# Opening of a two-layer decoder trunk: sums of squares with tokens on partitions, and the first weights split in two pieces

## Chip, cores, metric

The kernel runs on one core of one Trainium2 chip, in one launch. The metric is device time in microseconds (us). The engines are named as in the profile: PE (TensorE, matmuls; PEld are its weight loads), DVE (VectorE), ACT (ScalarE), POOL (GpSimd), SP (SyncE, which issues most transfers). "SPq" is SP's DMA queue.

## What is computed

A trunk of two layers on 512 tokens with 1024 features. Each layer normalizes its input, scales and shifts it by vectors computed from a conditioning vector c, projects it, mixes it three ways, and ends in a gated feed-forward part. The change concerns only the first normalization and the start of the first projection:

```python
c_act = silu(c)
mod = (c_act @ w_ada + b_ada)                   # six vectors of 1024: sh1, sc1, g1, sh2, sc2, g2
h = rmsnorm(x, norm1_w) * (1 + sc1) + sh1       # x * rsqrt(mean(x*x) + EPS) * norm1_w ...
u = h @ w_in                                    # the input projection
q = u[..., 1024:1536]                           # one of its parts; pool and conv inputs are others
```

## The kernel before

*Layout.* Features lie on partitions and tokens along the free axis: `x[k]` is slice k of the features (128 of 1024, k = 0 to 7) by 512 tokens. Weights arrive in blocks of 128x128 in the order in which they are used.

*Precision.* Every product is made of three matmuls in a reduced float format (`F32R`): an operand is split into a high half (rounded) and a low half (the rest), and `mm3` adds high x high, high x low and low x high. For weights `split_w` makes the halves: `whi` on ACT (line 402), then `wlo` on DVE (line 405). For the activations of the first normalization `first_scaled` (line 638, DVE) multiplies x by the column `am` and the row `rstd`, `first_hi` (line 642, ACT) adds the shift and rounds, `first_lo` (line 645, DVE) makes the low half.

*The opening.* While x arrives, `c` is turned into a column of silu values and spread to a row on all partitions (`csil`) by eight transposes (line 163 is the helper). PE runs idle matmuls (`WARM`, `WARM2`, on `ones`) between. Then, slice by slice, squares are made on DVE and ACT, pairs are added on DVE (line 881), and a matmul with a 128x128 matrix of ones sums over the partitions, so that the sum of squares of every token stands on all partitions. ACT takes the reciprocal root y of the 128x512 sums (line 888) and a scaled square of it (line 889); DVE makes the Newton step from them in two instructions (lines 893, 894), which leaves `rstd` (with a negative sign; `minus` and `abias` carry the sign to the other side).

*Modulation.* For each slice j, `ada_first` makes two dots of 1024 elements with `csil` on DVE (line 482, each followed by the read of its accumulator), for the scale (SC1) and the shift (SH1), and finishes them on ACT: `am` (line 506) and `mod` (line 509). The rows of the matrix for it come by `ada_first_load`, two transfers of 512 KB for each slice; six tiles hold them.

*Weights of the first loop.* For each slice k the loop over k reads one chunk of 7 blocks (448 KB): four blocks for q and three for other inputs. In the loop a step has 21 matmuls: four token tiles of q with three each, then three feature tiles with three each. Three `raw` tiles hold chunks on arrival.

*Order.* Each engine runs its queue in order. The order is that of the compiler's plan: an instruction wrapped in `pin` stays behind everything that was written before it for its engine; the others (the `whi` splits, `am` and `mod` of slices from 1 on, `first_hi`, the transfers) are placed where the plan takes their operands to be ready. `tc.issue_after(ins)` puts an instruction behind `ins` in the queue of the same engine; it is no wait. `split_after` and `fetch_after` hold such marks: the split of a slice's weights stands behind the previous slice's `first_hi` on ACT; the fetches, which SP issues, are marked behind DVE instructions (`step`).

Of the kernel before, what the change touches and what calls it, by code (L numbers as in the profile page):

```python
# [12 lines left out]
F32 = mybir.dt.float32  # L13
F32R = mybir.dt.float32r
BF16 = mybir.dt.bfloat16
I32 = mybir.dt.int32
AF = mybir.ActivationFunctionType
ALU = mybir.AluOpType
# [3 lines left out]
P = 128  # L22
D = 1024
S = 512
L = 2
KT = D // P
# [3 lines left out]
TT = S // P  # L30
# [5 lines left out]
BLOCK = 256  # L36
DFF = 2816
NF = DFF // P
EPS = 1e-6
NEG = -1e30  # L40
SCALE = 1.0 / math.sqrt(HD)
C_BLOCKS = 8
# [13 lines left out]
C_N1, C_N2, C_ADA, C_PS, C_CW = 0, 8, 16, 64, 66  # L56
# [9 lines left out]
SH1, SC1, G1, SH2, SC2, G2 = range(6)  # L66
# [9 lines left out]

WARM = 9

WARM2 = 19

GATE2 = ([("gate", j) for j in range(6)] + [("attn", 0), ("attn", 1), ("gate", 6), ("gate", 7)]
         + [("attn", j) for j in range(2, 8)])
# [3 lines left out]
def hybrid_trunk(ctx, tc, xT, ws, ada, cols, pool_w, qk_w, crow, pos, con, out):  # L86
    nc = tc.nc
    V, A, T = nc.vector, nc.scalar, nc.tensor

    const = ctx.enter_context(tc.tile_pool(name="const", bufs=1))  # L90
    big = ctx.enter_context(tc.tile_pool(name="big", bufs=BIG))
    wp = ctx.enter_context(tc.tile_pool(name="wp", bufs=4))
# [6 lines left out]
    def nm(s):  # L99
        uid[0] += 1  # L100
        return f"{s}{uid[0]}"

    def bigt(dt=F32R):
        return big.tile([P, S], dt, tag="big", name=nm("big"))
# [13 lines left out]
    def sm(shape, dt=F32, tag="sm", bufs=8):  # L118
        return small.tile(shape, dt, tag=tag, name=nm(tag), bufs=bufs)

    f32 = lambda ap: ap.bitcast(F32)
# [34 lines left out]
    def matmul(*a, **k):  # L156
        tc.keep_in_program_order(T.matmul(*a, **k))  # L157

    def pin(ins):
        return tc.keep_in_program_order(ins)  # L160

    def transpose(*a):
        tc.keep_in_program_order(T.transpose(*a))  # L163
# [11 lines left out]
    def cut(pair, *ix):  # L175
        return pair[0][ix], pair[1][ix]

    def table(func, after):

        A.activation(sm([P, 1], tag="tab", bufs=1), after, func)  # L180
# [6 lines left out]
    x = [const.tile([P, S], F32, name=f"x{k}") for k in range(KT)]  # L187
    colt = const.tile([P, L, NCOL], F32, name="colt")
# [15 lines left out]
    ident = const.tile([P, P], F32, name="ident")  # L204
# [3 lines left out]
    ones = f32(ones_r)  # L208
# [4 lines left out]
                            base=0, pattern=[[-1, P]], channel_multiplier=1)  # L213
    epst = const.tile([P, 1], F32, name="epst")
    nc.gpsimd.memset(epst, EPS)

# [20 lines left out]
    def fetch(tile, l, blocks):  # L239
        for i, n, src in runs(l, blocks):  # L240
            nc.sync.dma_start(tile[:, i:i + n].rearrange("p b n -> p (b n)"), src)
# [134 lines left out]
    items = []  # L376
    for l in range(L):
# [8 lines left out]
        for blocks in first_part + list(feed_forward()):  # L386
            if not isinstance(blocks, list):
                if isinstance(blocks, int):
                    blocks = GateUp(l, blocks)
# [3 lines left out]
    at = [0, 0]  # L393
    loaded = deque()
    hold, dots_after, last_split, scaled = [None], [None], [None], [None]

    def rawt():
        return wp.tile([P, C_BLOCKS, P], F32, tag="raw", name=nm("raw"), bufs=RAW)
# [33 lines left out]
    split_after, last_hi = [None], [None]  # L432

    fetch_after = [None]

    def load_w():
        while at[1] < min(at[0] + 1 + SUMS_AHEAD, len(items)):
            sums, sub = items[at[1]]
            if sums is not None and sub == 0:
                sums.begin()  # L440
            at[1] += 1
        sums, what = items[at[0]]
        at[0] += 1
        if sums is not None:
            return sums.load(what)
        l, blocks = what
        raw = rawt()
        with tc.issue_after(fetch_after[0].ins) if fetch_after[0] is not None else nullcontext():
            fetch(raw, l, blocks)
        if by_transfer(l, blocks):  # L450
            return split_by_transfer(raw, l, blocks)
        with tc.issue_after(split_after[0].ins) if split_after[0] is not None else nullcontext():
            return split_w(raw, len(blocks))

    ahead_now = [4]

    def next_w(ahead=None):
# [8 lines left out]
    def wrow(w, b0):  # L466
        return (w[0][:, b0:b0 + 4, :].rearrange("p b n -> p (b n)"),
                w[1][:, b0:b0 + 4, :].rearrange("p b n -> p (b n)"))
# [19 lines left out]
    def ada_first_load(j, after=None, parts=(SC1, SH1)):  # L488
        tiles = {}
        for part in parts:  # L490
            tiles[part] = w4([P, D])
            with issued_after(after):
                nc.sync.dma_start(tiles[part], ada[0, part, j])
        return tiles

    first_dots = {}


    abias = const.tile([P, KT], F32, name="abias")
    minus = const.tile([P, KT], F32, name="minus")  # L500

    def ada_first(j, tiles, part):
        first_dots[j, part] = pin(ada_dot(tiles[part], 0, part, j))
        m = mod[0][:, part, j:j + 1]
        if part == SC1:
            ins = A.activation(amod[0][0][:, j:j + 1], m, AF.Identity, scale=minus[:, j:j + 1],
                               bias=abias[:, j:j + 1])
        else:
            ins = A.activation(m, m, AF.Identity, bias=colt[:, 0, C_ADA + part * KT + j:C_ADA + part * KT + j + 1])
        if j == 0:  # L510

            pin(ins)
# [343 lines left out]
    for i in range(WARM):  # L856
# [4 lines left out]
        if i == 6:  # L861
            for j in range(KT):
                transpose(rows[j // 4][:, j % 4 * P:(j % 4 + 1) * P], ccol[:, j:j + 1].to_broadcast([P, P]), ident)
        matmul(scratch[:, 1, :P], ones, ones, start=True, stop=True)

    first = [ada_first_load(0, None, (SC1,))]
    step = []
    pin(V.tensor_scalar(minus, colt[:, 0, C_N1:C_N1 + KT], -1.0, None, op0=ALU.mult))
    pin(V.scalar_tensor_tensor(abias, colt[:, 0, C_ADA + SC1 * KT:C_ADA + (SC1 + 1) * KT], 1.0,
                               minus, op0=ALU.add, op1=ALU.mult))  # L870
    sq = [bigt(F32) for _ in range(KT)]
    for k in range(KT):
        if k == 0 or (k % 2 == 1 and k < KT - 1):
            step.append(pin(V.tensor_mul(sq[k], x[k], x[k])))  # L874
        else:
            if k in (2, 4):
                h = k // 2 - 1
                pin(A.activation(csil[:, h * S:(h + 1) * S], rows[h], AF.Copy))
            pin(A.activation(sq[k], x[k], AF.Square))
        if k % 2 == 1:  # L880
            step.append(pin(V.tensor_add(sq[k], sq[k - 1], sq[k])))  # L881
            matmul(scratch[:, 0], ones, sq[k], start=(k == 1), stop=(k == KT - 1))
    first[0].update(ada_first_load(0, step[3], (SH1,)))
    idle = ps_mm()
    for _ in range(WARM2):
        matmul(idle[:, :P], ones, ones, start=True, stop=True)
    y, y2, t = bigt(F32), bigt(F32), bigt(F32)
    A.activation(y, scratch[:, 0], AF.Abs_reciprocal_sqrt, bias=epst, scale=1.0 / D)
    split_after[0] = A.activation(y2, y, AF.Square, scale=(0.5 / D) ** 0.5)
    ada_first(0, first[0], SC1)  # L890
    ada_first(0, first[0], SH1)

    pin(V.scalar_tensor_tensor(t, scratch[:, 0], D * EPS, y2, op0=ALU.add, op1=ALU.mult))  # L893
    pin(V.scalar_tensor_tensor(norm.rstd, t, 1.5, y, op0=ALU.subtract, op1=ALU.mult))  # L894
    norm.first_scaled(0)
    norm.first_hi(0)
    fetch_after[0] = step[4]
    loaded.append(load_w())
    split_after[0] = last_hi[0]
    norm.first_lo(0)  # L900
    first.append(ada_first_load(1, step[6]))
    ada_first(1, first[1], SC1)
    norm.first_scaled(1)
    ada_first(1, first[1], SH1)
    norm.first_hi(1)
    fetch_after[0] = step[7]
    loaded.append(load_w())
    split_after[0] = last_hi[0]
    norm.first_lo(1)
    first.append(ada_first_load(2, first_dots[0, SC1]))  # L910
    fetch_after[0] = first_dots[0, SH1]
    with tc.issue_after(last_hi[0].ins):
        for t, src in ((cont, con), (qkw, qk_w), (post, pos)):
            A.dma_start(t, src)
# [2 lines left out]
    for l in range(L):  # L917
# [7 lines left out]
        for n, (k, lo, hi) in enumerate([(k, 0, S) for k in range(KT)] if l == 0 else HALVES + REST):  # L925
            if l == 0:
                if k + 3 < KT:
                    first.append(ada_first_load(k + 3, first_dots[0, SH1]))
                if k + 2 < KT:
                    ada_first(k + 2, first[k + 2], SC1)  # L930
                    ada_first(k + 2, first[k + 2], SH1)
                    norm.first_scaled(k + 2)
                    norm.first_hi(k + 2)
                loaded.append(load_w())
                split_after[0] = last_hi[0] if k + 2 < KT else None
                fetch_after[0] = None
                if k + 2 < KT:
                    norm.first_lo(k + 2)
            if k not in held:
                held[k] = next_w(0 if l == 0 else (2, 1)[n] if n < 2 else None)  # L940
            if l > 0 and n == 3:
                bulk.extend(later)
                bulk_rate[0] = 0.75
            w = held[k]
            h = norm.k(k)
            for t in range(lo // P, hi // P):
                if (l > 0, n, t) == (True, 1, 1):
                    second(norm, l, 0, bank)
                mm3(q_ps[t], cut(h, slice(None), slice(t * P, (t + 1) * P)), wrow(w, 0), k == 0, k == KT - 1)
            for z in range(3):  # L950
                mm3(f_ps[z][:, lo:hi], wblk(w, 4 + z), cut(h, slice(None), slice(lo, hi)),
                    k == 0 and lo == 0, k == KT - 1)
# [633 lines left out]
```

## Time and profile before

| | us |
|---|---|
| median of 3 runs | 1436.25 |
| lowest, highest | 1435.33, 1436.51 |
| profiled execution, its whole time | 1436.01 |
| its span in the profile | 1434.2 |

Busy in that span: PE 1427.7 us, DVE 1039.6, ACT 731.9, POOL 153.2. The granted PE clock is full throughout.

How to read the rows: a timeline row gives the start and the duration in us, the engine, the line of the kernel, the operation, the tile written and the tiles read (buffer numbers left out), their shapes, and the number of instructions merged in the row; in square brackets stands how long the engine had been idle before it and what ended the wait. A row of the chain gives start, duration and what the chain lay on. A row with a stretch "A:B" gives the busy time (and instruction count) of PE, PEld, DVE, ACT and POOL in it, PE's granted clock, the busy share of the DMA engines and their GB/s. Matmuls overlap, so a row's duration is longer than the step from one matmul to the next.

### The profile page before, as it was taken

To read this page: it belongs to the slowest core of one execution; us is meant where nothing else is said; L and a number is where in the kernel's file an instruction comes from. 1 tells how busy PE (TensorE), PEld (TensorE's weight loads), DVE (VectorE), ACT (ScalarE), POOL (GpSimd) and SP (SyncE) were. 2 spreads that over 40 slices of the span, in tenths; PEclk is the share of its full clock that TensorE was granted. 3 is DMA by queue.
4 is the path that set the end of the run, shared out by engine and by line. 5 is a ranking of instruction groups with operands and counts; after the bars stand their busy time and mean duration, and the time that the engine had idled before them with its cause. 6 is when DMAs were issued, how large, how long until landed. Compare 5 with 4: busy or idle time off the path is not lost.

```text
span 1434.2 us, 21999 instructions
## 1 busy us (share of the span) xinstructions
PE 1427.7 (100%) x8322; PEld 1256.7 (88%) x8322; DVE 1039.6 (72%) x1903; ACT 731.9 (51%) x1229; POOL 153.2 (11%) x215
## 2 busy tenths in 40 slices
PE   9999999999999999999999999999999999999999
PEld 7888888888988998989988878888889989999997
DVE  8887777648686767667789986665878747657663
ACT  5645666634553452535454675666336525435450
POOL 0000110101100310211001000010020103111200
PEclk9999999999999999999999999999999999999999
DMA  9647876674346766746527655566772527646522
GB/s 351 216 146 215 222 181 171 175 237 158 96 130 220 198 172 204 191 141 207 189 87 250 170 151 145 135 162 168 262 212 85 140 104 192 174 112 171 141 86 83
DMA packets 92378, 245.51 MB, mean 171 GB/s; under 512 B 11752, under 2 KB 24432, under 8 KB 92272
## 3 DMA queue, kind: packets, MB, share of 16 engines
q1 hardware_dynamic: 67312, 177.37, 35.9%
q0 software_dynamic: 24368, 66.60, 22.7%
q8 instruction: 65, 1.06, 0.3%
q14 instruction: 41, 0.34, 0.1%
q10 hardware_dynamic: 592, 0.14, 0.0%
HBM read 241.97 MB, written 2.10 MB: 170 GB/s over the span
## 4 chain that ended last, share of the span: by engine, by line
PE 97%; DVE 1%; DMA 1%; issue 1%; ACT 0%; ACTq 0%; DVEq 0%; POOLq 0%
PE mm L157 83%; PE pair L157 11%; PE mm L163 2%; DMA wlo<-in_ws 1%; DVE wlo L405 0%; DMA colt<-in_cols 0%; DVE big L874 0%; DVE big L881 0%; DVE wlo L416 0%; DVE big L645 0%; DVE w L482 0%; DVE tmp L638 0%; ACT big L642 0%; DVE big L894 0%; DVE big L893 0%
## 5 line engine op out<-in xcount | busy, mean ns | idle before, releaser
L157 PE MATMUL mm<-big,whi 128*128 128x512 f32 (+1 forms) x4350 | 1077.8, 339 | 0.0
L157 PEld LDWEIGHTS mm<-big,whi 128*128 128x128 f32 x4350 | 744.4, 190 | 85.9 <-issue 2.6
L157 PE MATMUL mm<-big,wlo 128*128 128x512 f32 (+1 forms) x2175 | 735.2, 338 | 0.4 <-DMA wlo<-in_ws 0.4
L157 PEld LDWEIGHTS mm<-big,wlo 128*128 128x128 f32 x2175 | 412.6, 190 | 45.7 <-issue 0.8
L402 ACT ACTIVATE whi<-raw 128x1024 fp32r<-128x1024 f32 (+2 forms) x191 | 197.0, 1034 | 202.4 <-PE mm L157 108.8
L405 DVE TENSOR_TENSOR wlo<-raw,whi 128x1024 fp32r<-128x1024 f32 (+2 forms) x191 | 224.7, 1187 | 43.1 <-ACT whi L402 42.6
L402 ACT ACTIVATE whi<-w 128x1024 fp32r<-128x1024 f32 x78 | 82.5, 1058 | 148.6 <-PE mm L157 88.4
L1273 DVE SCALAR_TENSOR_TENSOR x<-mm,mod,x 128x512 f32<-128x512 f32 (+1 forms) x89 | 61.6, 695 | 73.8 <-PE mm L157 73.5
L405 DVE TENSOR_TENSOR wlo<-w,whi 128x1024 fp32r<-128x1024 f32 x78 | 94.0, 1221 | 29.1 <-ACT whi L402 28.5
L482 DVE SCALAR_TENSOR_TENSOR w<-w,csil 128x1024 f32<-128x1024 f32 x80 | 95.9, 1223 | 16.9 <-DMA w<-in_ada 16.8
L263 POOL DMA_DIRECT2D w<-in_ws x72 | 46.3, 656 | 483.3 <-DVE wlo L405 228.7
L426 POOL DMA_DIRECT2D wlo<-in_ws x47 | 40.2, 854 | 402.8 <-ACT wlo L424 254.5
L157 PE MATMUL pair<-whi,big 128*128 128x512 f32 x240 | 79.9, 389 | 0.0
L265 POOL DMA_DIRECT2D w<-in_ws x72 | 63.9, 906 | 141.4 <-DMA w<-in_ws 139.4
L157 PE MATMUL pair<-big,whi 128*128 128x256 f32 (+1 forms) x376 | 74.0, 294 | 0.0
L422 ACT ACTIVATE whi<-raw 128x1024 fp32r<-128x1024 f32 x47 | 50.1, 1066 | 32.9 <-PE mm L157 20.3
L157 PEld LDWEIGHTS pair<-big,whi 128*128 128x128 f32 x376 | 60.4, 191 | 2.2
L157 PE MATMUL pair<-big,wlo 128*128 128x256 f32 (+1 forms) x188 | 55.3, 294 | 0.0
L157 PEld LDWEIGHTS pair<-whi,big 128*128 128x128 f32 x240 | 45.1, 188 | 9.2
L1230 DVE SCALAR_TENSOR_TENSOR big<-big,mm 128x512 f32<-128x512 f32 x48 | 32.7, 684 | 25.5 <-PE mm L157 24.9
L424 ACT ACTIVATE wlo<-whi 128x1024 fp32r<-128x1024 f32 x47 | 49.6, 1057 | 0.5
L656 DVE TENSOR_TENSOR big<-tmp,big 128x512 fp32r<-128x512 f32 x48 | 33.0, 691 | 22.0 <-ACT big L655 21.0
(237 smaller groups left out, 1400.8 us busy)
## 6 DMA issues: line engine op xcount, KB each, us to landing
raw<-in_ws SPq DMA_DIRECT2D x146, 512.0 KB, 4.3
w<-in_ada SPq DMA_DIRECT2D x80, 512.0 KB, 5.7
w<-in_ws POOLq DMA_DIRECT2D x144, 256.0 KB, 4.7
wlo<-in_ws POOLq DMA_DIRECT2D x47, 512.0 KB, 6.9
raw<-in_ws SPq DMA_DIRECT2D x64, 256.0 KB, 3.7
raw<-in_ws SPq DMA_DIRECT2D x24, 384.0 KB, 3.8
raw<-in_ada SPq DMA_DIRECT2D x16, 512.0 KB, 4.3
raw<-in_ws SPq DMA_DIRECT2D x16, 448.0 KB, 5.3
```

The costliest lines, as they stand in the source:

```text
L157: tc.keep_in_program_order(T.matmul(*a, **k))
L263: nc.gpsimd.dma_start(dst, self.source(0, 1))
L265: nc.gpsimd.dma_start(dst, self.source(*other), accum_op=ALU.add)
L402: A.activation(hi[:, :n], raw[:, :n], AF.Copy)
L405: ins = V.tensor_sub(lo[:, :n], raw[:, :n], f32(hi)[:, :n])
L422: A.activation(hi[:, :n], raw[:, :n], AF.Copy)
L424: A.activation(lo[:, :n], f32(hi)[:, :n], AF.Copy, scale=-1.0)
L426: nc.gpsimd.dma_start(lo[:, i:i + m].rearrange("p b n -> p (b n)"), src, accum_op=ALU.add)
L482: return V.scalar_tensor_tensor(aw, aw, 1.0, csil, op0=ALU.mult, op1=ALU.mult, accum_out=mod[l][:, part, j:j + 1])
L656: last_split[0] = V.tensor_sub(lo, src, f32(hi))
L1230: V.scalar_tensor_tensor(sg, sg, 1.0, branch, op0=ALU.add, op1=ALU.mult)
L1273: V.scalar_tensor_tensor(x[k][:, lo:hi], src, mod[l][:, part, k:k + 1], x[k][:, lo:hi], op0=ALU.mult, op1=ALU.add)
```

## The change

Six edits, all in the opening and the first two steps of the first loop:

1. The squares of the last slice, and the last add, are made in two halves of 256 tokens. The sums over features are taken with the data as the stationary operand and one column of ones as the moving one: four matmuls per pair of slices, each with one output column, so that tokens lie on partitions and the sums of all 512 tokens are a 128x4 tile (`stat`).
2. The root and the Newton step run on 128x4: two ACT instructions (y, and t = -0.5 (mean + EPS)), then four on GpSimd. The four columns are spread back by four transposes into PSUM, where `rstd` stays. The sign handling (`minus`) goes; `abias` moves behind the third pair of slices.
3. The 19 idle matmuls become 5 ahead of the transposes and 7 behind them.
4. The first weight chunk (`load_first`) is split in two pieces, four blocks and three, and the first slice's high and low half stand between them in the code.
5. In the first two steps of the loop q's matmuls run by kind, four token tiles at a time (`q_first`): high x high, high x low of the weights, then low x high.
6. The marks on the fetches are left out, and in slice 1 the two dots stand together ahead of the scaling.

```diff
-WARM2 = 19
+WARM2 = 5, 7
...
+    def q_first(o, h, w, start):
+        for z, (a, b) in enumerate(((0, 0), (0, 1), (1, 0))):
+            for t in range(TT):
+                matmul(o[t], h[a][:, t * P:(t + 1) * P], wrow(w, 0)[b], start=start and z == 0, stop=False)
...
+    hepst = const.tile([P, 1], F32, name="hepst")
+    nc.gpsimd.memset(hepst, -0.5 * EPS)
...
+    def load_first():
...
+        n, cuts = len(blocks), (slice(0, 4), slice(4, len(blocks)))
+        raw = rawt()
+        fetch(raw, l, blocks)
...
+        for i, b in enumerate(cuts):
+            pin(A.activation(hi[:, b], raw[:, b], AF.Copy))
+            pin(V.tensor_sub(lo[:, b], raw[:, b], f32(hi)[:, b]))
+            if i == 0:
+                norm.first_hi(0)
+                norm.first_lo(0)
+        return hi, lo
...
-    first = [ada_first_load(0, None, (SC1,))]
-    step = []
-    pin(V.tensor_scalar(minus, colt[:, 0, C_N1:C_N1 + KT], -1.0, None, op0=ALU.mult))
+    first = [ada_first_load(0, None, (SC1, SH1))]
...
+    def token_sums(src, ts, start=False, stop=False):
+        for t in ts:
+            matmul(stat[:, t:t + 1], src[:, t * P:(t + 1) * P], ones[:, :1], start=start and t == 0, stop=stop and t == TT - 1)
...
-            matmul(scratch[:, 0], ones, sq[k], start=(k == 1), stop=(k == KT - 1))
-    first[0].update(ada_first_load(0, step[3], (SH1,)))
...
+    for h in range(2):
+        c = slice(h * BLOCK, (h + 1) * BLOCK)
+        square(KT - 1, c)
+        pin(V.tensor_add(sq[KT - 1][:, c], sq[KT - 2][:, c], sq[KT - 1][:, c]))
+        token_sums(sq[KT - 1], range(2 * h, 2 * h + 2), stop=True)
...
-    A.activation(y, scratch[:, 0], AF.Abs_reciprocal_sqrt, bias=epst, scale=1.0 / D)
-    split_after[0] = A.activation(y2, y, AF.Square, scale=(0.5 / D) ** 0.5)
+    warm(WARM2[0])
+    y, t, r = [sm([P, TT], tag="rst", bufs=3) for _ in range(3)]
+    pin(A.activation(y, stat, AF.Abs_reciprocal_sqrt, bias=epst, scale=1.0 / D))
+    pin(A.activation(t, stat, AF.Identity, bias=hepst, scale=-0.5 / D))
     ada_first(0, first[0], SC1)
+    nc.gpsimd.tensor_mul(t, t, y)
+    nc.gpsimd.tensor_mul(t, t, y)
+    nc.gpsimd.tensor_scalar(t, t, 1.5, None, op0=ALU.add)
+    nc.gpsimd.tensor_mul(r, t, y)
+    norm.rstd = scratch[:, 1]
+    for i in range(TT):
+        transpose(norm.rstd[:, i * P:(i + 1) * P], r[:, i:i + 1].to_broadcast([P, P]), ident)
+    warm(WARM2[1])
     ada_first(0, first[0], SH1)
-    pin(V.scalar_tensor_tensor(t, scratch[:, 0], D * EPS, y2, op0=ALU.add, op1=ALU.mult))
-    pin(V.scalar_tensor_tensor(norm.rstd, t, 1.5, y, op0=ALU.subtract, op1=ALU.mult))
     norm.first_scaled(0)
-    norm.first_hi(0)
-    fetch_after[0] = step[4]
-    loaded.append(load_w())
-    split_after[0] = last_hi[0]
-    norm.first_lo(0)
-    first.append(ada_first_load(1, step[6]))
+    loaded.append(load_first())
+    first.append(ada_first_load(1))
     ada_first(1, first[1], SC1)
+    ada_first(1, first[1], SH1)
     norm.first_scaled(1)
-    ada_first(1, first[1], SH1)
     norm.first_hi(1)
-    fetch_after[0] = step[7]
     loaded.append(load_w())
     split_after[0] = last_hi[0]
     norm.first_lo(1)
...
-            for t in range(lo // P, hi // P):
+            if l == 0 and k < 2:
+                q_first(q_ps, h, w, k == 0)
+            for t in range(lo // P, hi // P) if l > 0 or k >= 2 else ():
```

More of the change, by code (lines that the diff above doesn't have):

```diff
@@ L453, in load_w @@
             return split_w(raw, len(blocks))
+    def load_first():
+        _, (l, blocks) = items[at[0]]
+        at[0] += 1
+        n, cuts = len(blocks), (slice(0, 4), slice(4, len(blocks)))
+        raw = rawt()
+        fetch(raw, l, blocks)
+        hi = wp.tile([P, C_BLOCKS, P], F32R, tag="whi", name=nm("whi"), bufs=5)
+        lo = wp.tile([P, C_BLOCKS, P], F32R, tag="wlo", name=nm("wlo"), bufs=5)
+        for i, b in enumerate(cuts):
[5 more added lines that the diff above has]
+        return hi, lo
     ahead_now = [4]
@@ L499, in hybrid_trunk @@
     abias = const.tile([P, KT], F32, name="abias")
-    minus = const.tile([P, KT], F32, name="minus")
     def ada_first(j, tiles, part):
@@ L505, in ada_first @@
         if part == SC1:
-            ins = A.activation(amod[0][0][:, j:j + 1], m, AF.Identity, scale=minus[:, j:j + 1],
+            ins = A.activation(amod[0][0][:, j:j + 1], m, AF.Identity, scale=colt[:, 0, C_N1 + j:C_N1 + j + 1],
                                bias=abias[:, j:j + 1])
@@ L864, in hybrid_trunk, with square @@
         matmul(scratch[:, 1, :P], ones, ones, start=True, stop=True)
-    first = [ada_first_load(0, None, (SC1,))]
-    step = []
-    pin(V.tensor_scalar(minus, colt[:, 0, C_N1:C_N1 + KT], -1.0, None, op0=ALU.mult))
-    pin(V.scalar_tensor_tensor(abias, colt[:, 0, C_ADA + SC1 * KT:C_ADA + (SC1 + 1) * KT], 1.0,
-                               minus, op0=ALU.add, op1=ALU.mult))
-    sq = [bigt(F32) for _ in range(KT)]
-    for k in range(KT):
+    first = [ada_first_load(0, None, (SC1, SH1))]
+    sq = [bigt(F32) for _ in range(KT)]
+    stat = scratch[:, 0, :TT]
+    def token_sums(src, ts, start=False, stop=False):
+        for t in ts:
+            matmul(stat[:, t:t + 1], src[:, t * P:(t + 1) * P], ones[:, :1], start=start and t == 0, stop=stop and t == TT - 1)
+    def square(k, c=slice(0, S)):
         if k == 0 or (k % 2 == 1 and k < KT - 1):
-            step.append(pin(V.tensor_mul(sq[k], x[k], x[k])))
+            pin(V.tensor_mul(sq[k], x[k], x[k]))
         else:
@@ L878, in hybrid_trunk @@
                 pin(A.activation(csil[:, h * S:(h + 1) * S], rows[h], AF.Copy))
-            pin(A.activation(sq[k], x[k], AF.Square))
-        if k % 2 == 1:
-            step.append(pin(V.tensor_add(sq[k], sq[k - 1], sq[k])))
-            matmul(scratch[:, 0], ones, sq[k], start=(k == 1), stop=(k == KT - 1))
-    first[0].update(ada_first_load(0, step[3], (SH1,)))
-    idle = ps_mm()
-    for _ in range(WARM2):
-        matmul(idle[:, :P], ones, ones, start=True, stop=True)
-    y, y2, t = bigt(F32), bigt(F32), bigt(F32)
@@ L888, in hybrid_trunk @@
-    A.activation(y, scratch[:, 0], AF.Abs_reciprocal_sqrt, bias=epst, scale=1.0 / D)
-    split_after[0] = A.activation(y2, y, AF.Square, scale=(0.5 / D) ** 0.5)
-    ada_first(0, first[0], SC1)
+            pin(A.activation(sq[k][:, c], x[k][:, c], AF.Square))
+    for k in range(0, KT - 2, 2):
+        square(k)
+        square(k + 1)
+        pin(V.tensor_add(sq[k + 1], sq[k], sq[k + 1]))
+        token_sums(sq[k + 1], range(TT), start=k == 0)
+    pin(V.scalar_tensor_tensor(abias, colt[:, 0, C_ADA + SC1 * KT:C_ADA + (SC1 + 1) * KT], 1.0,
+                               colt[:, 0, C_N1:C_N1 + KT], op0=ALU.add, op1=ALU.mult))
@@ new lines, in hybrid_trunk, with warm @@
+    square(KT - 2)
+    for h in range(2):
[3 more added lines that the diff above has]
+        token_sums(sq[KT - 1], range(2 * h, 2 * h + 2), stop=True)
+    idle = ps_mm()
+    def warm(n):
+        for _ in range(n):
+            matmul(idle[:, :P], ones, ones, start=True, stop=True)
+    warm(WARM2[0])
+    y, t, r = [sm([P, TT], tag="rst", bufs=3) for _ in range(3)]
+    pin(A.activation(y, stat, AF.Abs_reciprocal_sqrt, bias=epst, scale=1.0 / D))
@@ L909, in hybrid_trunk @@
     norm.first_lo(1)
-    first.append(ada_first_load(2, first_dots[0, SC1]))
-    fetch_after[0] = first_dots[0, SH1]
+    first.append(ada_first_load(2))
     with tc.issue_after(last_hi[0].ins):
```

## The prediction, made before the changed kernel was run

> **What bounds the kernel now.** I read the chain that ended last first, by engine, then its opening in order of time.
>
> ```profile
> PE 97%; DVE 1%; DMA 1%; issue 1%; ACT 0%; ACTq 0%; DVEq 0%; POOLq 0%
> ```
>
> ```profile
> 22.86 0.50 PE mm L157
> 23.36 2.07 PE pair L157 x9
> 25.43 2.73 PE mm L157 x12
> ```
>
> TensorE (PE) carries 97% of the chain, so only what moves PE's stream counts. The last hand-over to PE in the opening is at 22.86 us; from there the chain stays on PE through the first input loop. One step of that loop (one 128-row slice k of D) is 21 matmuls, 2.07 + 2.73 = 4.80 us, some 0.23 us per matmul. A gain in the opening reaches the end only if PE is still ahead at the *last* point where the new kernel makes it wait, and the end moves by what it is ahead there. That point need not be the first matmul. Next, DVE, ACT and PE in the opening's timeline.
>
> ```profile
> 10.12 0.69 DVE L881 TENSOR_TENSOR big<-big,big 128x512 f32<-128x512 f32 x1 [0.26 <-ACT big L879]
> 10.74 1.23 DVE L482 SCALAR_TENSOR_TENSOR w<-w,csil 128x1024 f32<-128x1024 f32 x1
> 11.89 0.08 DVE L482 DVE_READ_ACCUMULATOR w<-w,csil 128x1 f32 x1
> 12.03 1.23 DVE L482 SCALAR_TENSOR_TENSOR w<-w,csil 128x1024 f32<-128x1024 f32 x1
> 13.18 0.08 DVE L482 DVE_READ_ACCUMULATOR w<-w,csil 128x1 f32 x1
> 13.48 0.69 DVE L893 SCALAR_TENSOR_TENSOR big<-pair,big 128x512 f32<-128x512 f32 x1 [0.22 <-ACT big L889]
> 14.21 0.69 DVE L894 SCALAR_TENSOR_TENSOR big<-big,big 128x512 f32<-128x512 f32 x1
> 15.02 0.75 DVE L638 SCALAR_TENSOR_TENSOR tmp<-x,am,big 128x512 f32<-128x512 f32 x1
> ```
>
> ```profile
> 9.46 0.63 ACT L879 ACTIVATE big<-x 128x512 f32<-128x512 f32 x1 [0.26 <-DMA x<-in_xT]
> 12.10 0.69 ACT L888 ACTIVATE big<-pair,epst 128x512 f32<-128x512 f32 x1 [2.01 <-PE pair L157]
> 12.81 0.63 ACT L889 ACTIVATE big<-big 128x512 f32<-128x512 f32 x1
> 13.35 0.37 ACT L506 ACTIVATE am<-mod,abias,minus 128x1 f32<-128x1 f32 x1
> 13.63 0.28 ACT L509 ACTIVATE mod<-mod,colt 128x1 f32<-128x1 f32 x1
> ```
>
> ```profile
> 16.64 0.50 PE L157 MATMUL mm<-whi,big 128*128 128x512 f32 x1 [0.40 <-ACT big L642]
> ```
>
> The last slice of x lands at 9.46; sums, root, rstd and scaling (15.02) follow in series, and the first real matmul starts at 16.64. Last, slice k=2 on ACT, DVE and PE, and the transfer behind it.
>
> ```profile
> 21.29 0.72 ACT L642 ACTIVATE big<-tmp,mod 128x512 fp32r<-128x512 f32 x1
> ...
> 23.92 0.96 ACT L402 ACTIVATE whi<-raw 128x896 fp32r<-128x896 f32 x1 [1.91 <-DMA raw<-in_ws]
> 24.78 0.37 ACT L506 ACTIVATE am<-mod,abias,minus 128x1 f32<-128x1 f32 x1
> ```
>
> ```profile
> 23.86 1.22 DVE L482 SCALAR_TENSOR_TENSOR w<-w,csil 128x1024 f32<-128x1024 f32 x1
> 25.01 0.08 DVE L482 DVE_READ_ACCUMULATOR w<-w,csil 128x1 f32 x1
> 25.19 0.75 DVE L638 SCALAR_TENSOR_TENSOR tmp<-x,am,big 128x512 f32<-128x512 f32 x1
> 25.85 1.08 DVE L405 TENSOR_TENSOR wlo<-raw,whi 128x896 fp32r<-128x896 f32 x1
> 26.86 0.75 DVE L645 SCALAR_TENSOR_TENSOR big<-tmp,mod,big 128x512 fp32r<-128x512 f32 x1
> ```
>
> ```profile
> 27.76 0.40 PE L157 MATMUL mm<-whi,big 128*128 128x512 f32 x1
> ```
>
> ```profile
> 13.67 0.42 SPq L241 DMA_DIRECT2D raw<-in_ws  x1
> ```
>
> ```profile
> 10.00:24.00 14.00, 13.43 (x70) 10.03 (x71) 12.88 (x20) 5.87 (x12) 0.00 (x0) 1.00 1.03 410
> ```
>
> ACT stands 1.91 us for the weights of slice 2, which were issued at 13.67 and land at 23.9. The DMA engines run full (share 1.03, 410 GB/s) all that while. Behind that weight split, on ACT's queue, stands the small `am` (24.78); then come on DVE the scaling (25.19), `wlo` (25.85) and the low half (26.86, ending 27.61). PE's third matmul of slice 2 needs that low half and starts at 27.76: PE's own pace and DVE arrive together.
>
> **The change, part by part.** *Loads.* Taking the marks off would count if they held anything. They tie SP's loads to DVE instructions, and the trace shows no hold: the first weights went out at 6.36, before the add (7.77) that they are marked behind.
>
> ```profile
> 6.36 0.54 SPq L241 DMA_DIRECT2D raw<-in_ws  x1
> ```
>
> ```profile
> 7.77 0.69 DVE L881 TENSOR_TENSOR big<-big,big 128x512 f32<-128x512 f32 x1
> ```
>
> SP's order (x, then for each slice two modulation rows and the weights) is the same before and after, so transfers keep their times. *Squares.* `minus` goes and `abias` moves behind the slices. Both stood ahead of the squares, but the end of this part waits for x's last slice at 9.46 anyway: 0. In halves, the last square and add overlap. DVE takes 0.69 at 512 columns and 1.08 at 896, so about 0.43 at 256, and ACT's 0.63 becomes about 0.41: 9.46 + 0.41 + 0.43 + 0.40 for the second half = 10.7, against 10.81. Gain 0.1. *Sums.* Old: 1.29 us from the add's end to ACT at 12.10. New: one-column matmuls per token tile; behind the last add two remain, four passes.
>
> ```profile
> 11.83 4.40 PE L157 MATMUL mm<-ones 128*128 128x128 f32 x38
> ```
>
> ```profile
> 3.57 0.27 PE L163 MATMUL pair<-ident,c 8*128 8x8 f32 x1
> ```
>
> ```profile
> 3.88 0.18 ACT L859 ACTIVATE ccol<-pair 128x8 f32<-128x8 f32 x1 [1.02 <-PE pair L163]
> ```
>
> A pass over 128 columns costs 4.40/38 = 0.116; over one column it lies between 0 and that. I take 0.116, since the weight load stays: 0.46, plus 0.31 from a tiny matmul's start to ACT (3.57 to 3.88). So ACT starts at 11.5. The root and the -0.5 form are two small ACT ops at the 0.28 pitch of `am` and `mod`: 12.1. *GpSimd.* Four ops on 128x4, none of them in the trace. Bounds from its own rows, and the transposes' row:
>
> ```profile
> 1.50 0.09 POOL L215 MEMSET epst<- 128x1 f32 x1
> 1.62 0.29 POOL L212 TENSOR_SCALAR_AFFINE_SELECT mask<-mask 128x128 f32<-128x128 f32 x1
> ```
>
> ```profile
> L265 POOL DMA_DIRECT2D w<-in_ws x72 | 63.9, 906 | 141.4 <-DMA w<-in_ws 139.4 <-issue 1.4 <-DVE w L482 0.4
> ```
>
> ```profile
> 4.69 1.92 PE L163 MATMUL mm<-ident,ccol 128*128 128x128 f32 x8
> ```
>
> 0.09 to 0.91 us each; I take 0.2, between the two compute rows, since the width is that of the first and there are two inputs, plus 0.04 for each hand-over (ACT ends at 13.44, DVE starts at 13.48): 1.0 in all, so 13.1. Nothing else is queued on POOL there. The new memset on POOL lies in its idle start: 0. Four transposes at 1.92/8 = 0.24, plus 0.1: the scaling of slice 0 can start at T = 14.2, since the second dot is over at 13.26. Before: 15.02. The two DVE steps at 13.48 and 14.21 and ACT's square at 12.81 go. The five and seven idle matmuls (0.23 each) fill PE's waits and end before its operands come: 0.
>
> Here a page bears on the GpSimd step. The second dot, 12.03 to 13.26, reads two SBUF tiles, and no row here shows a reading GpSimd op beside such a DVE op. The Trainium skill, "SBUF — State Buffer", section "Who interferes with whom", says that a VectorE instruction with two SBUF inputs and a GpSimd instruction that reads SBUF block each other, a whole instruction long. By that rule GpSimd would start at 13.26 and T would be 15.3; by the rows alone T is 14.2; the sum below comes out the same either way.
>
> *Split in two, q first.* After T: scaling 0.75, then the high half on ACT at its 0.72, and 0.1 of hand-overs. PE starts at T + 1.57 = 15.8 instead of 16.64. It then has eight matmuls, 1.8 us, to do before it needs the low half, so its small stalls within slices 0 and 1 go too. DVE: first weight piece beside ACT, low half from T + 1.57 (0.67 from start to start), second piece 0.5, free at T + 2.74. Slice 1: two dots at 1.15, scaling 0.67, `wlo` 1.0, low half 0.67, together 4.64. Slice 2: two dots, 2.3. So DVE is free for the scaling of slice 2 at T + 9.68 = 23.9, 1.3 ahead of 25.19. Reading rstd from PSUM costs about what SBUF does (0.69 at 13.48 against 0.75 at 15.02): 0.
>
> *What is late next.* That scaling also needs `am`, and `am` stands behind the weight split that waits for the DMA. Slice 2's weights still go out when the modulation rows ahead of them get their buffers back from the first two dots (13.26), whose times don't change, and the queue ahead of them is full. So they land at 23.9 again, `am` runs at 24.78, the scaling at 25.19, the low half ends at 27.61, and PE's third matmul of slice 2 can start at 27.65 instead of 27.76. **Sum: -0.1 us.** Later slices give nothing: PE ran unbroken from there before. The profiled execution took 1436.01 (its span 1434.2 and 1.8 around it), so 1435.9; the median of the runs, 1436.25, is 0.24 above it, so 1436.1.
>
> **The rivals.** *(a) `am` goes ahead of the split on ACT.* ACT's order is the compiler's plan. In the old one the split of slice 2 stands right behind the previous high half (21.29, then 23.92), and `am` after it. The plan is made anew, and a DVE that is 1.3 us ahead makes `am` ready at 22.7, before the weights. Then the scaling starts at 23.9, `wlo` waits for the split (24.9), the low half ends at 26.65 and PE is 1.05 ahead: 1435.2 (with T at 15.3 0.2 ahead, 1436.0). Against it: a planner that lets ACT wait 1.91 us for a transfer takes it as landing early. *(b) The weights of slice 2 land sooner as well*, by 1 us. Then DVE alone is the limit: scaling at 23.9, then 0.67, 1.0 and 0.75 to the low half's end at 26.3, and PE is 1.4 ahead: 1434.8. For it: 10.2 us, from 13.67 to 23.9, is long for one transfer; against it: a full queue in the same order. *(c) Slower: the GpSimd chain.* T may slip to 25.19 - 9.68 = 15.5 at no cost; beyond that each us costs a us. If the dot blocks it, 15.5 is reached at about 0.25 us per op; at 0.91, the dearest POOL row, T is 13.26 + 4 x 0.95 + 1.06 = 18.1 and 2.6 us are lost: 1438.9. For it: no row of a small GpSimd arithmetic op; against it: the compute rows of 0.09 to 0.29. *(d) PE does not start sooner*, because the second weight piece (0.5) and the rule above take the 0.84 away. The wait at slice 2 hides that: 1436.1 again.
>
> **How the numbers follow.** A difference under 0.2% (2.9 us) can hardly be told from no change. The whole stretch before the first matmul is 16.6 us, and all cases but the far end of (c) stay within that. Chances: forecast with (d) 0.58, (a) 0.22, (b) 0.08, (c) 0.09, of which a third beyond 0.2%, unforeseen 0.03. Range: down to (b) and a little for the runs' own spread, 1434.7; up to (c) with 0.45 us per op (T 16.3 when blocked, 0.8 lost), 1436.9, with the same little on top, 1437.1. Faster 0.03, same 0.94, slower 0.03.
>
> **What would show it.** Right: the first real matmul at 15.5 to 16.9, the scaling of slice 0 at 14.2 to 15.3, GpSimd ops near 0.2; ACT waiting for slice 2's weights until about 23.9 with `am` behind it; PE unbroken from about 27.7. Wrong: `am` of slice 2 ahead of the split, slice 2's weights before 23.3, GpSimd ops over 0.3, or a PE wait behind slice 2.

## The result, and the profile after

The changed kernel takes 1446.17 us (median of 6 runs, 1445.62 to 1446.86), the kernel before 1436.38 (6 runs): a ratio of 1.0069 [1.0058, 1.0079], 9.8 us slower. The forecast was 1436.1 and its range ended at 1437.1. The profiled execution took 1446.21, its span 10.2 us more than before.

Where do 10.2 us come from in a kernel that is 99% PE? First the totals of the page after, then the group of matmuls that carries an idle time (the last column: idle before the group, and what ended it).

```profile
span 1444.4 us, 22043 instructions
...
PE 1431.3 (99%) x8336; PEld 1263.3 (87%) x8336; DVE 1038.3 (72%) x1902; ACT 730.7 (51%) x1231; POOL 155.6 (11%) x220
...
L157 PE MATMUL pair<-whi,big 128*128 128x512 f32 x240 | 80.3, 394 | 7.5 <-DVE tmp L661 7.5
```

PE's busy time grew by 3.6 us (from 1427.7), so the larger part of the 10.2 is idle time, and one row names it: matmuls that write a tile named `pair` waited 7.5 us for the DVE instruction that scales x (line 661, `first_scaled`). That is strange at first sight: a matmul of the first slice has no operand from that instruction. PE, then DVE, in the timeline:

```profile
18.20 0.48 PE L157 MATMUL mm<-whi,big 128*128 128x512 f32 x1
18.51 0.63 PE L157 MATMUL pair<-whi,big 128*128 128x512 f32 x2
26.63 0.79 PE L157 MATMUL pair<-whi,big 128*128 128x512 f32 x1 [7.49 <-DVE tmp L661]
...
31.41 0.40 PE L157 MATMUL mm<-big,wlo 128*128 128x512 f32 x1
...
33.00 0.39 PE L157 MATMUL mm<-whi,big 128*128 128x512 f32 x1
...
37.76 0.39 PE L157 MATMUL mm<-whi,big 128*128 128x512 f32 x1
```

```profile
16.19 0.75 DVE L661 SCALAR_TENSOR_TENSOR tmp<-x,am,pair 128x512 f32<-128x512 f32 x1 [2.60 <-PE pair L163]
...
21.21 0.74 DVE L661 SCALAR_TENSOR_TENSOR tmp<-x,am,pair 128x512 f32<-128x512 f32 x1
...
25.83 0.74 DVE L661 SCALAR_TENSOR_TENSOR tmp<-x,am,pair 128x512 f32<-128x512 f32 x1
```

The scalings read `tmp<-x,am,pair`; before it was `x,am,big`. `rstd` now lies in `scratch[:, 1]`, one half of a PSUM pair. The other half, `scratch[:, 0]`, is `pair_b[:, 0]`: the accumulator of q's fourth token tile. So q's fourth matmul, the first of q that writes this pair, stands until the scaling of slice 2 (25.83 to 26.57) has read the pair. The scaling of slice 2 is the last one that stands before the first slice's matmuls in the code. Between 21.95, the end of slice 1's scaling, and 25.83 nothing reads the pair, and PE stands all the same: a clash of a read and a write in the same moment would not hold it there.

After the wait the matmuls are slow as well: the eleven from 26.63 to 31.41 take 0.43 us each, not 0.23. The granted clock (the column behind the five engines) in the stretches of the opening:

```profile
10.00:11.00 1.00, 0.99 (x8) 0.99 (x9) 0.79 (x3) 0.52 (x2) 0.00 (x0) 0.91 1.02 418
11.00:12.00 1.00, 1.00 (x6) 1.00 (x6) 0.93 (x2) 0.00 (x0) 0.00 (x0) 0.50 1.03 417
...
16.00:18.00 2.00, 2.00 (x13) 2.00 (x12) 1.56 (x3) 0.97 (x2) 0.00 (x0) 0.59 1.04 414
18.00:20.00 2.00, 1.14 (x7) 0.66 (x6) 2.00 (x3) 1.01 (x2) 0.00 (x0) 1.00 1.02 399
...
22.00:24.00 2.00, 0.00 (x0) 0.00 (x0) 2.00 (x3) 0.72 (x1) 0.00 (x0) 1.00 0.98 361
24.00:26.00 2.00, 0.00 (x0) 0.00 (x0) 2.00 (x5) 1.20 (x3) 0.00 (x0) 0.62 1.05 373
...
28.00:30.00 2.00, 2.00 (x6) 1.54 (x5) 2.00 (x4) 0.59 (x2) 0.00 (x0) 0.50 0.78 269
...
32.00:34.00 2.00, 2.00 (x11) 1.65 (x10) 2.00 (x3) 0.52 (x1) 0.00 (x0) 1.00 0.90 334
```

It was full in the whole profile of before. After, it is halved twice: from about 10.8 to 17.7, while the sums, the root and the transposes run, and from about 24.5 to 31.3, behind the long wait. The Trainium skill, "TensorE: Matmul & The Clock Gate", part "The HAM clock gate", says that the clock is halved after an idle window of about 3.4 us and given back after as long a busy one. The second drop agrees: PE's last matmul ahead of the wait ends at 19.14, the clock falls at 24.5 and is back 4.7 us after the next one starts (26.63). The first does not follow from what the profile counts as busy: PE shows 0.99 and 1.00 there.

The account, from PE's first real matmul to its first of slice 2 (at full clock 21 matmuls take 37.76 − 33.00 = 4.76 us, 0.227 each). Before, slice 2 began here:

```profile
27.30 0.39 PE L157 MATMUL mm<-whi,big 128*128 128x512 f32 x1
```

| | us |
|---|---|
| first real matmul later: 18.20 − 16.64 | +1.56 |
| wait of the fourth matmul | +7.49 |
| eleven matmuls at half clock: 4.78 − 11 x 0.227 | +2.28 |
| the last matmul ahead of the wait running out, and a slower first step (the remainder) | +0.26 |
| small stalls of before that are gone: (27.30 − 16.64) − 42 x 0.227 | −1.13 |
| slice 2 begins later: 37.76 − 27.30 | +10.46 |

Little of it is given back later: the span is 10.2 us longer. The long run of 87 matmuls behind the first loop's opening, in the chain that ended last, starts 10.43 us later than before and takes the same 19.72; the fence has the row of before, then that of after.

```profile
54.02 19.72 PE mm L157 x87
```

```profile
64.45 19.72 PE mm L157 x87
```

### The profile page after: what moved, and what is told of

Read it like the earlier page. It is cut to its first block, busy times and chain, and to the rows that moved or that the text cites. A ratio compares the mean times of both kernels' runs of the same rounds, so it can differ in the third digit from the quotient of the medians.

```text
span 1444.4 us, 22043 instructions
## 1 busy us (share of the span) xinstructions
PE 1431.3 (99%) x8336; PEld 1263.3 (87%) x8336; DVE 1038.3 (72%) x1902; ACT 730.7 (51%) x1231; POOL 155.6 (11%) x220
## 3 DMA queue, kind: packets, MB, share of 16 engines
q8 instruction: 65, 1.06, 0.3%
## 4 chain that ended last, share of the span: by engine, by line
PE 97%; DMA 1%; DVE 1%; issue 1%; SPq 0%; ACT 0%; DVEq 0%; POOLq 0%; ACTq 0%
PE mm L157 84%; PE pair L157 12%; PE mm L163 2%; DMA wlo<-in_ws 1%; DMA x<-in_xT 0%; DVE w L506 0%; DVE tmp L661 0%; DVE big L668 0%; DVE big L899 0%; DVE big L909 0%; SPq L203 0%; DVE wlo L412 0%; PE pair L163 0%; ACT big L665 0%; DVE x L1314 0%
## 5 line engine op out<-in xcount | busy, mean ns | idle before, releaser
L1271 DVE SCALAR_TENSOR_TENSOR big<-big,mm 128x512 f32<-128x512 f32 x48 | 32.6, 683 | 24.5 <-PE mm L157 23.9
```

What stands on the lines that cost most here:

```text
L1271: V.scalar_tensor_tensor(sg, sg, 1.0, branch, op0=ALU.add, op1=ALU.mult)
```

## The experiments

The theory ("W"): the shared pair makes the wait, and the wait the second drop of the clock; what remains of the change is worth nothing or a little. The rivals: PSUM itself, or the transposes into it, are the cost; the split weights or the new order of q are; or the slow opening is.

**e1: `rstd` copied out of PSUM.** The first scaling reads PSUM, all others a copy in SBUF.

```diff
                 norm.first_hi(0)
+                pin(A.activation(rstd_sb, norm.rstd, AF.Copy))
+                norm.rstd = rstd_sb
...
-    norm.rstd = scratch[:, 1]
+    rstd_sb, norm.rstd = norm.rstd, scratch[:, 1]
```

> The changed kernel with one ACT instruction more: behind the first high half, rstd is copied from PSUM to SBUF, and the scalings of slices 1 to 7 read the copy. Theory W (PE's fourth matmul of slice 0 waits 7.49 us because its output and rstd are the two halves of one PSUM tile, whose readers so far include the scaling of slice 2; the wait then drops PE's clock to half from 24.7 to 31.2): the wait goes, the second drop of the clock goes, the first real matmul stays at about 18.2, and with slice 2's low half at 28.2 instead of 27.6 the time is 1436.5 to 1437.5 us. Rival G (the new chain to rstd, with GpSimd and transposes, is what costs; the wait only absorbs what DVE owes anyway): the time stays above 1442.

Measured: 1437.18 (10 runs) against 1436.71, 1.0004 [0.9995, 1.0013]. PE's timeline:

```profile
18.16 0.50 PE L157 MATMUL mm<-whi,big 128*128 128x512 f32 x1 [0.18 <-ACT big L667]
18.50 0.87 PE L157 MATMUL pair<-whi,big 128*128 128x512 f32 x3
...
28.89 0.50 PE L157 MATMUL mm<-whi,big 128*128 128x512 f32 x1
```

Three matmuls to the pairs run through (18.50); the first one is as late as after the change, and the loss is all but gone. So the late first matmul is not the 10 us. PE's third matmul of slice 2, at 27.76 before, comes at 28.89.

**e2: the shared pair alone.** The kernel before, with one line added: the last DVE step of the root writes `rstd` into the pair's free half.

```diff
+    norm.rstd = scratch[:, 1]
     pin(V.scalar_tensor_tensor(norm.rstd, t, 1.5, y, op0=ALU.subtract, op1=ALU.mult))
```

> The kernel before with one edit: the DVE step that makes rstd writes it to the free half of the PSUM pair whose other half later takes q's fourth token tile. Theory W: PE waits there, now at its tenth matmul of slice 0 (18.75), until the scaling of slice 2 ends at about 25.9, some 7 us, with a dropped clock behind it: 1443 to 1446 us. Rival G (the new chain to rstd is the cause): within 1 us of before, 1435.5 to 1437.5.

Measured: 1444.29 (one run), 7.6 above 1436.71.

```profile
18.89 0.40 PE L157 MATMUL pair<-whi,big 128*128 128x512 f32 x1
25.70 0.79 PE L157 MATMUL pair<-whi,big 128*128 128x512 f32 x1 [6.42 <-DVE tmp L638]
```

Without any other part of the change the wait is there (the 7.6 is one run's; the 21 runs of before lie between 1435.24 and 1439.36). It is 6.42 long, and falls on the tenth matmul, not the fourth, because before each token tile had its three matmuls in turn. The long run of 87 matmuls starts at 62.11, 8.09 later than before; the 1.67 beyond the wait go with a clock of 0.50 from 24 to 30.

**e3: the same, later in the code.** After, but the loop's preparation of slice k+2 (dots, scaling, halves) is written behind the matmuls of slice k.

```diff
-            if l == 0:
...
-                    norm.first_scaled(k + 2)
-                    norm.first_hi(k + 2)
...
                 q_first(q_ps, h, w, k == 0)
...
+            if l == 0:
...
+                    norm.first_scaled(k + 2)
+                    norm.first_hi(k + 2)
...
```

> The changed kernel with each slice's matmuls written ahead of the preparation of the slice after next, so that only the scalings up to slice k+1 stand before them in the code; nothing is copied. Theory W in its strict form (the wait is drawn by the compiler from the order of the code, on the whole tile, not on the half that is written): the fourth matmul now waits for the scaling of slice 1, which ends at about 21.95, and not for that of slice 2 (26.57); PE saves 4.6 us of wait and some of the slow clock: 1439 to 1442 us. Rival H (the chip itself holds PE's write to one half while DVE reads the other): the wait stays as long as the scalings run one behind the other, no change, 1445 to 1447.

Measured: 1441.76 (one run), 5.05 above 1436.71.

```profile
17.95 0.63 PE L157 MATMUL pair<-whi,big 128*128 128x512 f32 x2
21.14 0.79 PE L157 MATMUL pair<-whi,big 128*128 128x512 f32 x1 [2.56 <-DVE tmp L661]
```

The scaling of slice 1 (20.34 to 21.08) now ends the wait, since it is the last one written ahead of slice 0's matmuls. The same matmul, the same tile, the same engines, another place in the code: the wait is put there by the program's order on the whole pair. The long run of 87 matmuls starts at 58.24, 4.22 later than before. The rest of the 5.05 comes behind the opening; the chain of this profile, as that of e4's, has a wait for a transfer (`w<-in_ada`, 7.34 us from 116.67) that before's has not, and its cause was not looked into. Whether the chip could have read one half while PE wrote the other was not tried.

**e5: a PSUM tile of its own.** `rstd` stays in PSUM, in another tile; the third feature accumulator takes the pair's free half in its place.

```diff
-    norm.rstd = scratch[:, 1]
+    norm.rstd = ps_mm()
...
-        f_ps = [ps_mm(), ps_mm(), ps_mm()]
+        f_ps = [ps_mm(), ps_mm(), ps_mm() if l > 0 else pair_b[:, 1]]
```

> The changed kernel with rstd in a PSUM tile of its own; the free half of the pair takes the third feature accumulator of the first loop instead. Nothing is copied and all scalings read PSUM. Theory W (the shared tile is the cause, not that rstd lies in PSUM): no wait of PE on a scaling, as with the copy; the first real matmul at 17.6 to 18.4, the low half of slice 2 at 27.8 to 28.4, 0.2 to 0.5 earlier than with the copy: 1436.4 to 1437.0 where before is 1436.4, that is 0 to 0.6 slower. Rival H (DVE's reads of PSUM hold PE's writes in other banks): over 1440.

Measured: 1436.82 (11 runs) against 1436.19, 1.0002 [0.9993, 1.0011].

```profile
17.61 0.48 PE L157 MATMUL mm<-whi,big 128*128 128x512 f32 x1
17.93 0.85 PE L157 MATMUL pair<-whi,big 128*128 128x512 f32 x3
```

No wait. PSUM, the transposes into it, the split weights and the new order of q are all still there. Sharing the pair is the cause of the loss. With T, the start of slice 0's scaling, at 15.90 instead of the forecast 14.2, the time is still level, as the slack that the prediction counts on (up to T = 15.5) covers most of it.

**e4: does the clock hold if PE has wider work?** e1, with four idle matmuls (128 columns each) behind the one-column sums of the first pair of slices, and four behind those of the second pair.

```diff
         token_sums(sq[k + 1], range(TT), start=k == 0)
+        if k < 4:
+            warm(4)
```

> The copy of the first of these kernels, and four idle matmuls of 128 columns behind each of the first two groups of one-column sums. Theory C (a stretch of one-column matmuls counts as idle for PE's clock, which fell to half from 10.9 to 17.3 us): the clock stays full, ACT's root starts at about 11.8 instead of 12.97, the scaling of slice 0 at 14.6 to 15.0 instead of 16.19; the time is then 1435.4 to 1436.4, set by the weights of slice 2. If GpSimd's four ops and the second dot block each other (the page's rule), the first of them starts only at 13.6, the scaling of slice 0 at about 15.8 and the time is 1436.2 to 1437.2. Rival: the clock falls all the same, and the time is that of the copy alone.

Measured: 1435.67 (11 runs) against 1436.71, 0.9995 [0.9986, 1.0004]: not told apart from before. The clock stays at 1.00 through the opening, but the root starts at 13.16 instead of the expected 11.8, because the idle matmuls, 1.14 us for each four, stand ahead of the sums in PE's queue.

```profile
11.00:12.00 1.00, 1.00 (x12) 1.00 (x10) 0.95 (x3) 0.00 (x0) 0.00 (x0) 1.00 1.04 423
```

```profile
13.16 0.26 ACT L931 ACTIVATE rst<-pair,epst 128x4 f32<-128x4 f32 x1 [3.08 <-PE pair L157]
```

This is the row to set beside the one of after for the same microsecond: PE is 1.00 busy in both, and the clock 1.00 here, 0.50 there. PE runs one-column passes in that microsecond in both; what differs is what it ran shortly before:

```profile
10.24 1.14 PE L157 MATMUL mm<-ones 128*128 128x128 f32 x8
11.22 1.84 PE L157 MATMUL pair<-ones,big 128*128 128x1 f32 x16
```

**e6: fewer idle matmuls.** e5, with two in place of e4's four.

```diff
         token_sums(sq[k + 1], range(TT), start=k == 0)
+        if k < 4:
+            warm(2)
```

> The kernel with rstd in a tile of its own, and two idle matmuls of 128 columns behind each of the first two groups of one-column sums (four in the earlier kernel, which held the clock but stood 1.1 us each ahead of the next sums). Theory C (clock and queue both count): the clock stays full, ACT's root starts at 12.2 to 12.6, the scaling of slice 0 at 15.0 to 15.4 and slice 2's low half ends near 27.1 to 27.5: 0.2 to 0.7 us faster than before. Rival: two are too few, the clock falls to half before 12 us, ACT's root starts at 12.9 or later and the time is that of the tile of its own alone.

Measured: 1437.15 (11 runs) against 1436.19, 1.0007 [0.9998, 1.0015]; no gain. The root started early (11.67), but GpSimd's first step then fell beside the second dot:

```profile
12.17 1.02 POOL L932 TENSOR_TENSOR rst<-rst,rst 128x4 f32<-128x4 f32 x1 [10.24 <-ACT rst L930]
13.26 0.20 POOL L933 TENSOR_TENSOR rst<-rst,rst 128x4 f32<-128x4 f32 x1
```

```profile
13.00:14.00 1.00, 0.10 (x1) 0.00 (x0) 0.14 (x2) 0.81 (x2) 0.75 (x4) 0.50 1.02 406
```

The dot ran from 11.90 to 13.13, and the step, 0.20 otherwise, ended at 13.19. The clock fell at about 12.3, while PE was still busy, and was 0.50 until about 19.1; PE ran out of work at 13.1 (0.10 busy from 13 to 14). Slice 0's scaling came at 15.35 and slice 2's low half ended at 27.39, both as expected, but PE itself was late: its first real matmul stood behind the seven idle ones at half clock.

```profile
17.86 0.77 PE L157 MATMUL mm<-whi,big 128*128 128x512 f32 x1
```

**e7: GpSimd beside the dots, by itself.** The kernel before, with eight small GpSimd multiplications (128x4, operands in SBUF) behind the last add; their result is not used.

> The kernel before with eight small GpSimd multiplications (128x4, two SBUF inputs, result unused) that become ready when the last add ends, at about 10.8, just as the first dot starts on DVE (10.74 to 11.9; the second 12.03 to 13.2). By the page's rule GpSimd stands until the first dot ends, about 12.0, gets an op or two in between the dots or holds the second dot up by 0.2 to 0.5, and is done after 13.3. Without such a rule the eight run from 10.9 at 0.28 each and are done at 13.1, with the dots where they were. The time stays within 0.5 us of before in both.

Measured: 1435.65 (one run) against 1436.19.

```profile
10.71 1.11 POOL L886 TENSOR_TENSOR prb<-big,ones 128x4 f32<-128x4 f32 x1 [8.79 <-DVE big L881]
11.89 3.13 POOL L886 TENSOR_TENSOR prb<-prb,ones 128x4 f32<-128x4 f32 x7
```

```profile
10.54 1.22 DVE L482 SCALAR_TENSOR_TENSOR w<-w,csil 128x1024 f32<-128x1024 f32 x1
...
11.69 1.23 DVE L482 SCALAR_TENSOR_TENSOR w<-w,csil 128x1024 f32<-128x1024 f32 x1
...
13.55 0.69 DVE L896 SCALAR_TENSOR_TENSOR big<-pair,big 128x512 f32<-128x512 f32 x1 [0.63 <-ACT big L892]
14.27 0.69 DVE L897 SCALAR_TENSOR_TENSOR big<-big,big 128x512 f32<-128x512 f32 x1
```

The first step stands until 0.06 us behind the first dot's end. The other seven take 3.13 us, where seven at the pace of 0.28 to 0.30 that they have after the change would take about 2.0. Taken one by one, the first of them (11.89) lasts 1.08, until 0.05 behind the second dot's end; the next five start every 0.28, two of them wholly beside line 896, which has one operand in PSUM; the last (14.44) lasts 0.58, until 0.06 behind line 897, which reads two SBUF tiles. The dots keep their 1.22 and 1.23.

**e8: the four GpSimd steps as three on DVE.** e6, with

```diff
-    nc.gpsimd.tensor_mul(t, t, y)
-    nc.gpsimd.tensor_mul(t, t, y)
-    nc.gpsimd.tensor_scalar(t, t, 1.5, None, op0=ALU.add)
-    nc.gpsimd.tensor_mul(r, t, y)
+    pin(V.tensor_mul(t, t, y))
+    pin(V.tensor_mul(t, t, y))
+    pin(V.scalar_tensor_tensor(r, t, 1.5, y, op0=ALU.add, op1=ALU.mult))
```

> The kernel with rstd in a tile of its own and two idle matmuls behind each of the first two groups of sums, and the four GpSimd steps made as three small DVE instructions on 128x4 between the two dots. Theory L (the GpSimd ops stand behind the second dot, which reads two SBUF tiles, and PE's clock falls in that gap): the three steps take 0.4 to 0.6 us from about 12.1, transposes start at about 12.7 instead of 14.1, PE keeps its full clock, the second dot ends 0.6 to 0.9 later, at 13.8, and the scaling of slice 0 starts at 14.0 to 14.5 instead of 15.35. Slice 2's low half then ends at 26.6 to 27.2 (27.61 before): 0.4 to 1.0 us faster than before, which five rounds may not resolve. Rival: the weights of slice 2, issued later by what the second dot loses, hold it at 27.6 or later: no gain.

Measured: 1435.35 (11 runs, 1434.19 to 1438.28) against 1436.30, 0.9995 [0.9986, 1.0005]: not told apart. In its profile the clock was 0.50 from about 10.9 to 17.7 all the same and the scaling of slice 0 came at 16.43, not at 14.0 to 14.5.

```profile
9.00:10.00 1.00, 1.00 (x11) 1.00 (x11) 0.82 (x4) 0.97 (x3) 0.00 (x0) 1.00 1.05 428
10.00:11.00 1.00, 1.00 (x11) 1.00 (x11) 0.92 (x3) 0.25 (x1) 0.00 (x0) 0.96 1.01 412
```

Before, PE was less busy at that place, and the clock held:

```profile
9.00:10.00 1.00, 0.73 (x3) 0.09 (x1) 0.76 (x2) 0.74 (x2) 0.00 (x0) 1.00 1.03 420
```

So gaps in PE's work are not what costs the clock at this place; what PE runs is. The runs of e8 differ among themselves in the clock: three had a mean granted clock of 1.000 and took 1434.19, 1434.44 and 1434.83; the other eight, at 0.997 to 0.999, have a median of 1436.29, though one of them took 1434.41. That was seen afterwards; what decides whether two idle matmuls hold the clock stays open.

## Why the prediction was wrong, step by step

**The step that failed: "Reading rstd from PSUM costs about what SBUF does ... : 0".** The read itself was priced right: a scaling takes 0.75 from PSUM, as it took from SBUF. What was left out is who else writes that tile. The working followed the queues of ACT, DVE, SP and POOL, but not PE as a writer of the tile that DVE reads. So the sentence that later slices give nothing, because PE ran unbroken before, was argued from the old kernel's waits. e2 shows that this edit alone costs 7.6 us, e1 and e5 that the change without it is level. No rival had this mechanism; the 0.03 for a slower time beyond 0.2% lay with GpSimd. The signs of being wrong that it listed look for a PE wait behind slice 2; the wait came in slice 0.

**A second effect without a term: the clock.** Every duration was taken from a kernel at full clock. The change replaces the 512-column sums by one-column matmuls and leaves fewer idle ones, and the clock falls to half at about 10.8. At the wait it falls again.

**The way to T, the scaling of slice 0.** Forecast 14.2 (15.3 if the dot blocks GpSimd), measured 16.19. The rows, in order of the path:

```profile
10.24 0.76 DVE L917 TENSOR_TENSOR big<-big,big 128x256 f32<-128x256 f32 x2 [0.21 <-ACT big L904]
```

```profile
10.01 2.86 PE L157 MATMUL pair<-ones,big 128*128 128x1 f32 x16 [0.43 <-DVE big L909]
12.73 2.48 PE L157 MATMUL mm<-ones 128*128 128x128 f32 x10
15.01 1.06 PE L163 MATMUL pair<-ident,rst 128*128 128x128 f32 x4
```

```profile
12.97 0.26 ACT L927 ACTIVATE rst<-pair,epst 128x4 f32<-128x4 f32 x1 [2.46 <-PE pair L157]
```

```profile
13.47 0.20 POOL L930 TENSOR_TENSOR rst<-rst,rst 128x4 f32<-128x4 f32 x1 [11.55 <-ACT rst L928]
...
14.34 0.20 POOL L933 TENSOR_TENSOR rst<-rst,rst 128x4 f32<-128x4 f32 x1
```

- The last add ends at 11.00, forecast 10.7.
- Sums: forecast 0.46 + 0.31 behind the add, measured 1.97 (11.00 to 12.97). Not four passes of 0.116 remained: at 11.00 PE was still in the sixteen passes of the last two groups (10.01 to 12.87), and eight of them were to start, 0.21 apart at half clock. This term, 2.6 times as long as forecast, is the largest error in T.
- The two ACT steps: forecast 0.6, measured 0.42.
- GpSimd: forecast 0.2 an op, measured 0.20 to 0.22. The hand-overs are not 0.04 but 0.08 to 0.10; the chain from ACT's end to the last op takes 1.15 against 1.0.
- Transposes: forecast 1.06 to T, measured 1.65 (14.54 to 16.19). The five idle matmuls, costed at nothing because PE's operands come later, take 2.48 at half clock and end last.
- The seven behind them do the same to the first real matmul: the high half is ready at 17.75, it starts at 18.20.

**GpSimd beside the dot.** The rule weighed in the prediction holds as far as it makes GpSimd wait: in e6 and e7 a small GpSimd step stood until 0.06 us behind the dot's end, 1.02 and 1.11 us long. After the change itself it played hardly a part: the first op began at 13.47, 0.11 before the dot's end, and took 0.20 like the others.

**What was right.** From T to the scaling of slice 2, forecast 9.68, measured 25.83 − 16.19 = 9.64. So the point from which a late T costs, 15.5, can be tested where the wait is gone, by PE's third matmul of slice 2 (27.76 before; one profile each):

| | T | T − 15.5 | third matmul later by |
|---|---|---|---|
| e6 | 15.35 | −0.15 | 0.77 |
| e4 | 15.56 | 0.06 | 0.14 |
| e5 | 15.90 | 0.40 | 0.25 |
| e8 | 16.43 | 0.93 | 0.78 |
| e1 | 16.54 | 1.04 | 1.13 |

In the last four, each us of T beyond that point costs about one, to within some 0.15 us, as rival (c) had it, though clock and sums made T late and not GpSimd. e6 does not fit: there PE, not DVE, came last, as it started at 17.86 and ran at half clock until 19.1. Rival (a)'s order on ACT did come: `am` of slice 2 at 24.80, ahead of the split at 25.09. Slice 2's weights, which the forecast had going out as before (13.67), went out at 14.76. With T this late, DVE's dots set the scaling of slice 2 and not the transfer, so the forecast's own limit, the split waiting for the DMA, never showed. The small stalls in slices 0 and 1 went (−1.13), but there the long wait had given the operands time; in e5 and e8, without the wait, (27.48 − 17.61) − 42 x 0.227 = 0.34 and (28.07 − 18.37) − 42 x 0.227 = 0.17 of them are left, so most went, as forecast.

## What to carry to other kernels

Before data is moved into a free half of a tile, list every later writer and reader of the *whole* tile in code order: the new wait appears where an engine that had nothing to do with the data writes the other half. A long wait on TensorE is charged twice here, once as the wait (7.49) and once as slow matmuls behind it (2.28). And where a change replaces wide matmuls by one-column ones, as here, durations of TensorE's work are to be taken at half clock too.

## What the runs showed of the hardware

Matmuls of one column leave PE busy in the profile and still lose the clock: 0.50 from about 10.8 to 17.7 after the change, 1.00 throughout in e4 with two groups of four 128-column matmuls between them. Groups of two were not enough in the profiles of e6 and e8.

Read in stretches of 0.1 us, the clock falls and comes back at 10.82 and 17.65, then at 24.48 and 31.30 after the change; at 9.38 and 16.20 in e1, 9.89 and 16.72 in e5, 12.32 and 19.14 in e6, 10.91 and 17.74 in e8. Each of these half-clock stretches is 6.82 or 6.83 us long. In e3 the changes are at 10.61, 17.44, 20.85 and 24.26, so the last two steps are 3.41, half of that. In these profiles, then, the changes within a run lie 3.41 us or a multiple of it apart, and the first fall comes at another place in each profile. Whether that is why some runs of e8 keep the clock was not tried.

In e3 the clock fell behind a wait of 2.56 us only, shorter than the idle window of the Trainium skill's page named above; there the measurement decides. The step from 17.44 to 20.85 still held 1.14 us of PE's work (until 18.58).

A blocked GpSimd step waits for the DVE instruction, and the DVE instruction does not wait for it: both dots in e7 kept their duration. The Trainium skill, "SBUF — State Buffer", section "Who interferes with whom", says that the order of issue decides who blocks. The two runs e6 and e7, in which the dot was first each time, agree, and none of these runs shows a small GpSimd step first beside a long dot.
